# A third buffer for raw expert weights in the dense stage, and seven buffers instead of eight for gathered rows of the second kind

## The chip, the cores and the metric

The kernel runs on one core of one Trainium2 chip. The metric is the device time of one execution in microseconds (us). The engines are named as in the profile: PE is TensorE (PEld its weight loads), DVE is VectorE, ACT is ScalarE, POOL is GpSimd, and SP is SyncE, whose queue issues plain DMAs. POOL issues the gathers.

## The reference, cut to what matters

One layer on 1024 tokens of width 1024: a mixing part (attention and a recurrence) and then the expert part, which this change touches. There are 16384 experts, each with a row `u` and a row `v` of 1024 numbers. Each token takes 8 heads x 16 experts:

```python
q = (xt @ w_query).reshape(TOKEN_BLOCK, PEER_HEADS, 2, PEER_HALF)
s = jnp.einsum('thpd,hpnd->thpn', q, sub_keys)
s_top, i_top = lax.top_k(s, K)
...
idx = jnp.take_along_axis(cand_idx, pos, axis=-1)
g = jax.nn.softmax(best, axis=-1)
u = expert_u[idx]
v = expert_v[idx]
act = jax.nn.gelu(jnp.einsum('td,thkd->thk', xt, u))
return jnp.einsum('thk,thkd->td', g * act, v)
```

## The kernel before, in words

The tokens form eight blocks of 128. Four of them (0, 5, 6, 7) are computed by gathering the chosen rows; the other four, 512 tokens in all, are computed densely, against all 16384 experts with a table of factors G that is zero where an expert was not chosen. The dense stage runs from about 1760 us to the end, and the gathers of token blocks 5, 6 and 7 are woven into it.

The dense stage goes through 128 blocks i of 128 experts. All matmuls use a high and a low part of each operand, three matmuls for one product. For block i the names are:

- `fetch` (line 1358) takes a buffer `raw` of 128x1024 floats (0.5 MB) and issues the DMA that fills it, with u(i) or v(i). `load` also splits it into high and low: a cast on ACT (line 104), a subtraction on DVE (line 105, "sub" below). The raw buffer is free after the subtraction. There are two of them for u and v together.
- `first(i)` is 24 matmuls into `ps_A` with the split `u` (two buffers), and a gelu on ACT into `a` (one buffer, line 1377).
- `weigh(i)` multiplies `a` with the factors on DVE (line 1392) and splits the product into `w` (four buffers): a cast on ACT, a subtraction on DVE.
- `second(g)`, after every fourth block, is 96 matmuls into `ps_y` that use four `w` and four `v`. The split `v` has four buffers, so v(4g+4) can be cast only when second(g) has ended.

PE's order in one group of four blocks is: first(4g+1), first(4g+2), first(4g+3), first(4g+4), second(g). Below, T stands for the end of a second, and the four firsts that follow it are called first 1 to first 4.

The gathers are steps in a list that `pump` works off, some three or four after each first and after each quarter of a second. A step of `gather_u` issues the gather of one row of `u` for 128 tokens (tile `g_u`, four buffers, line 1128) and takes the dot product of an earlier one on DVE (line 1134). A step of `gather_v` issues the gather of one row of `v` (tile `g_v`, GV buffers, line 1174); after every fourth, eight matmuls `g_y` (line 1188) use four gathered rows; the trace shows them as 16 records. Gathers go to POOL in order, and each also waits for the matmul that ended the last point of the pump.

In the first stretch of the dense stage (to about 2190 us) only `u` rows of block 5 are gathered, beside the routing of blocks 6 and 7 on DVE; from 2190 to 3240 us `u` rows and `v` rows by turns; from 3240 us `v` rows of block 7 alone. These are called the u stretch, the mixed stretch and the v stretch below.

On each engine instructions run in the order in which they stand in the program, and a scheduler sets that order when the program is built.

Of the kernel before, what the change touches and what calls it, by code (L numbers as in the profile page):

```python
# [9 lines left out]
F32 = mybir.dt.float32  # L10
# [16 lines left out]
DENSE = tuple(b for b in range(S // 128) if b not in GATHER)  # L27
TD = 128 * len(DENSE)
GC = 16
NGRP = 4  # L30
GU, GV, WB = 4, 8, 4
GUF = 3
BEHIND = 0, 1, 2, 3
FAST = 2
# [19 lines left out]
def b32(ap):  # L54
    return ap.bitcast(F32)
# [29 lines left out]
class Builder:  # L85
# [1013 lines left out]
    def after_part(self, p):  # L1099

        tbs = [tb for tb in range(p * 4, p * 4 + 4) if tb not in LATER]
        tbs = [tb for tb in tbs if tb in GATHER] + [tb for tb in tbs if tb in DENSE]
        rt = {tb: self.soon.pop(tb) if tb in self.soon else self.routed(tb) for tb in tbs}
        dense = sum([rt[tb] + self.table(tb) for tb in tbs if tb in DENSE], [])
        if p == 0:
            self.steps += rt[0] + self.merge(self.gather_u(self.blocks[0]) + self.sooner_v(self.blocks[0]), dense)
        else:
            n = len(rt[4])
            self.steps += dense[:n + 1] + self.merge(dense[n + 1:], rt[BRIDGE])
# [221 lines left out]
    def dense(self, da, db):  # L1331
        nc, I, tc = self.nc, self.I, self.tc
        NB = TD // 128
        groups = [(g, min(g + NGRP, 128)) for g in range(0, 128, NGRP)]
        points = (128 * -(-TD // 512) + len(groups) * NB) * RATE
        rate = (len(self.steps) - self.fast) / (points - self.fast / FAST)
        state = [0.0, self.fast]

        def pump(i, st):
            if state[1] > 0:  # L1340
                self.mark = [st.ins]
                self.pump(FAST)
                state[1] -= FAST
                return
            state[0] += rate
            n = int(state[0])
            state[0] -= n
            self.pump(n)
            self.mark = [st.ins]

        started = set()
        us, acts, Ws, Vs, Gs = {}, {}, {}, {}, {}


        def part(j, dk):
            return h2[j][dk // 4][:, dk % 4, :]

        def fetch(src):
            raw = raws.pop(0) if raws else db.tile([128, 1024], F32, tag="raw", bufs=2, name="raw")
            nc.sync.dma_start(raw, src)  # L1360
            return raw

        def load(src, pool, tag, bufs):
            raw = fetch(src)
            w = pool.tile([128, 2, 1024], F32R, tag=tag, bufs=bufs, name=tag)
            self.split(w[:, 0, :], w[:, 1, :], raw)
            return w

        def first(i):
            u = us.pop(i)  # L1370
            a = acts[i] = a0.pop() if a0 else db.tile([128, TD], F32, tag="a", bufs=1, name="a")
            np_ = -(-TD // 512)
            for c in range(np_):
                cs = slice(c * TD // np_, (c + 1) * TD // np_)
                ps = self.psum([128, TD // np_], "ps_A")
                st = self.lin(ps, u, lambda dk: (part(0, dk)[:, cs], part(1, dk)[:, cs]))
                nc.scalar.activation(a[:, cs], ps, AF.Gelu_apprx_tanh)
                pump(i, st)

        def factors(g):  # L1380
            lo, hi = groups[g]
            Gs[g] = da.tile([128, TD // GC, hi - lo, GC], F32, tag="G", bufs=2, name="Gt")
            nc.sync.dma_start(Gs[g].rearrange("j c i t -> j c (i t)"),
                              self.d_G[:, :, lo:hi, :].rearrange("c j i t -> j c (i t)"))

        def weigh(i):
            g, m = i // NGRP, i % NGRP
            if m == 0 and g + 1 < len(groups):
                factors(g + 1)
            a = acts.pop(i)  # L1390
            a3 = a.rearrange("p (c t) -> p c t", t=GC)
            nc.vector.tensor_tensor(a3, a3, Gs[g][:, :, m, :], op=ALU.mult)
            w = Ws[i] = da.tile([128, 2, TD], F32R, tag="w", bufs=WB, name="w")
            self.split(w[:, 0, :], w[:, 1, :], a)

        def second(g):
            lo, hi = groups[g]
            for tb in range(NB):
                cs = slice(tb * 128, (tb + 1) * 128)
                for hf in range(2):  # L1400
                    ds = slice(hf * 512, (hf + 1) * 512)
                    ps = self.psum([128, 512], "ps_y")
                    st = self.sum3(ps, [(Ws[i][:, 0, cs], Ws[i][:, 1, cs], Vs[i][:, 0, ds], Vs[i][:, 1, ds])
                                        for i in range(lo, hi)])
                    add(tb, hf, ps)
                pump(lo, st)

        def add(tb, hf, ps):
            ds = slice(hf * 512, (hf + 1) * 512)
            if (tb, hf) in started:  # L1410
                nc.vector.tensor_tensor(yac[tb][:, ds], yac[tb][:, ds], ps, op=ALU.add)
            else:
                nc.scalar.copy(yac[tb][:, ds], ps)
            started.add((tb, hf))


        h2 = [[None, None], [None, None]]
        acc = lambda i: db.tile([128, 1024], F32, name=f"yac{i}")

        def half(j, k):  # L1420
            h2[j][k] = db.tile([128, 4, TD], F32R, name=f"dh{j}{k}")

        yac = [acc(i) for i in range(2)]
        raws = [db.tile([128, 1024], F32, tag="raw", bufs=2, name="raw") for _ in range(2)]
        yac.append(acc(2))
        half(0, 0)
        half(1, 0)
        yac.append(acc(3))
        half(1, 1)
        us[0] = load(I["uT"][0], db, "u", 2)  # L1430
        a0 = [db.tile([128, TD], F32, tag="a", bufs=1, name="a")]
        half(0, 1)
        yac += [acc(i) for i in range(4, NB)]

        for j in range(4):
            nc.sync.dma_start(b32(h2[j % 2][j // 2]), self.d_h2T[j % 2][:, (j // 2) * 4:(j // 2) * 4 + 4, :])
        factors(0)
        for i in range(128 + 1):
            if i + 1 < 128:
                us[i + 1] = load(I["uT"][i + 1], db, "u", 2)  # L1440
            if i < 128:
                first(i)
            if i % NGRP == 0 and i or i == 128:
                second((i - 1) // NGRP)
            if i < 128:
                Vs[i] = load(I["expert_v"][i * 128:(i + 1) * 128, :], da, "v", NGRP)
                weigh(i)
        for n in range(NB):
            self.finish(db, DENSE[n], yac[n], "raw", 2)

    def run(self):
        tc = self.tc
# [95 lines left out]
```

## Time and profile before

| what | value |
|---|---|
| time, median of 3 runs | 3584.61 us (3577.67 to 3598.39) |
| the profiled execution's own time | 3616.83 us |
| its span, from the first instruction to the last | 3615.1 us |
| PE busy | 3196.5 us, 88% of the span |
| DVE busy | 2326.8 us, 64% |
| POOL busy | 1375.2 us, 38% |
| ACT busy | 1192.0 us, 33% |
| moved by DMA | 915.68 MB, 253 GB/s over the span |

A busy share is a mean over stages with different limits. Matmuls are pipelined, so each record is longer than the distance from one to the next.

### The profile page before, as it was taken

Reading aid. Unit: us, or ns where it says so; the run is one execution under the profiler, and the core shown is the slowest. Engines: PE = TensorE matmul, PEld = TensorE weight load, DVE = VectorE, ACT = ScalarE, POOL = GpSimd, SP = SyncE. Lnnn points to the kernel's source line nnn. Section 1 sums busy time; section 2 is a strip of 40 time slices with the busy share of each in tenths; the row PEclk is TensorE's granted clock in tenths of the full one; section 3 lists DMA queues with packets and bytes.
Section 4 is the critical chain, followed back from the end, with each engine's and each line's share of the span. In section 5 each row is a group of like instructions: output and inputs, shape, how many; then the busy total and the mean of one; then the engine's idle time right before and its main releaser. Section 6 shows DMA issues by size and latency. Waiting matters only on the chain.

```text
span 3615.1 us, 43218 instructions
## 1 busy us (share of the span) xinstructions
PE 3196.5 (88%) x15408; PEld 2320.3 (64%) x15408; DVE 2326.8 (64%) x5465; ACT 1192.0 (33%) x1860; POOL 1375.2 (38%) x1180
## 2 busy tenths in 40 slices
PE   6899989587878998897697899998989988899997
PEld 4477778465655665565476776665767666666665
DVE  5535557988778644678788776665666565664334
ACT  4437444266425631333332222222222121222121
POOL 0000013134445456431144445555545555554440
PEclk8899999888999999998898999999999999999998
DMA  8422445166776676763788889998999999898995
GB/s 312 161 81 94 135 138 160 58 211 223 265 264 202 230 250 204 242 201 112 247 266 265 288 278 346 340 372 316 351 331 354 344 335 329 312 350 307 346 326 186
DMA packets 392144, 915.68 MB, mean 253 GB/s; under 512 B 162148, under 2 KB 180708, under 8 KB 388088
## 3 DMA queue, kind: packets, MB, share of 16 engines
q0 software_dynamic: 149504, 536.94, 41.9%
q1 hardware_dynamic: 242424, 375.97, 31.9%
q8 instruction: 121, 1.98, 0.2%
q14 instruction: 95, 0.78, 0.1%
HBM read 851.70 MB, written 61.10 MB: 252 GB/s over the span
## 4 chain that ended last, share of the span: by engine, by line
PE 37%; DMA 25%; DVE 19%; issue 11%; ACT 4%; POOL 3%; another core or an unknown queue 0%; SPq 0%; DVEq 0%; POOLq 0%; ACTq 0%
DMA raw<-in_uT 9%; DMA g_u<-in_expert_u,g_ei 5%; DMA raw<-in_expert_v 4%; DVE g_u L1134 3%; PE ps_G L1302 2%; PE ps_y L692 2%; DMA g_u<-in_expert_u,ei 2%; PE ps_y L695 2%; PE g_y L1188 2%; PE ps_y L693 2%; PE h_y L1222 2%; DVE v L105 2%; POOL g_u L1146 2%; PE ps_A L692 1%; PE ps_A L693 1%
## 5 line engine op out<-in xcount | busy, mean ns | idle before, releaser
L1134 DVE CUSTOM_DVE_ANT_0 g_u<-g_u,g_h 128x1024 f32<-128x1024 f32 x384 | 463.9, 1221 | 149.1 <-DMA g_u<-in_expert_u,g_ei 112.2
L692 PE MATMUL ps_A<-dh,u 128*128 128x512 f32 x1024 | 433.3, 423 | 100.6 <-ACT u L104 89.7
L692 PE MATMUL ps_y<-v,w 128*128 128x512 f32 x1024 | 412.9, 403 | 36.2 <-ACT w L104 27.1
L693 PE MATMUL ps_A<-dh,u 128*128 128x512 f32 x1024 | 422.7, 413 | 8.0 <-DMA dh<-d_h2T 8.0
L1128 POOL DMA_INDIRECT g_u<-in_expert_u,g_ei x256 | 298.6, 1167 | 309.3 <-issue 100.8
L693 PE MATMUL ps_y<-v,w 128*128 128x512 f32 x1024 | 404.6, 395 | 0.0
L1174 POOL DMA_INDIRECT g_v<-in_expert_v,g_eT x256 | 284.8, 1112 | 255.0 <-PE g_y L1188 101.4
L1209 POOL DMA_INDIRECT h_v<-in_expert_v,g_eh x256 | 273.6, 1069 | 283.1 <-PE h_y L1222 212.8
L105 DVE TENSOR_TENSOR u<-raw,u 128x1024 fp32r<-128x1024 f32 x128 | 156.7, 1224 | 326.9 <-ACT u L104 308.9
L104 ACT CAST u<-raw 128x1024 fp32r<-128x1024 f32 x128 | 134.0, 1047 | 659.7 <-DMA raw<-in_uT 620.3
L692 PEld LDWEIGHTS ps_A<-dh,u 128*128 128x128 f32 x1024 | 206.9, 202 | 198.0 <-ACT u L104 110.9
L1128 POOL DMA_INDIRECT g_u<-in_expert_u,ei x128 | 163.2, 1275 | 341.9 <-DVE oneA L1295 103.7
L104 ACT CAST v<-raw 128x1024 fp32r<-128x1024 f32 x128 | 134.3, 1049 | 451.7 <-PE ps_y L695 252.4
L695 PE MATMUL ps_y<-v,w 128*128 128x512 f32 x1024 | 279.7, 394 | 0.3 <-DVE w L105 0.3
L692 PEld LDWEIGHTS ps_y<-v,w 128*128 128x128 f32 x1024 | 195.2, 191 | 124.4 <-issue 36.9
L105 POOL TENSOR_TENSOR whl<-wraw,whl 128x1024 fp32r<-128x1024 f32 x16 | 40.6, 2539 | 585.5 <-ACT whl L104 585.4
L1146 POOL DMA_INDIRECT g_u<-in_expert_u,g_ei x128 | 152.6, 1192 | 282.4 <-DVE g_act L1154 116.3
L695 PE MATMUL ps_A<-dh,u 128*128 128x512 f32 x1024 | 253.1, 389 | 0.8 <-DVE u L105 0.8
L104 ACT CAST whl<-wraw 128x1024 fp32r<-128x1024 f32 (+2 forms) x152 | 151.1, 995 | 297.1 <-PE ps_pb L695 55.2
L693 PEld LDWEIGHTS ps_A<-dh,u 128*128 128x128 f32 x1024 | 206.9, 202 | 52.8 <-DMA dh<-d_h2T 9.0
L105 DVE TENSOR_TENSOR whl<-wraw,whl 128x1024 fp32r<-128x1024 f32 (+2 forms) x136 | 155.2, 1142 | 116.1 <-ACT whl L104 112.7
L695 PEld LDWEIGHTS ps_y<-v,w 128*128 128x128 f32 x1024 | 194.6, 190 | 46.3 <-DVE w L105 4.0
(375 smaller groups left out, 6818.7 us busy)
## 6 DMA issues: line engine op xcount, KB each, us to landing
raw<-in_uT SPq DMA_DIRECT2D x128, 512.0 KB
raw<-in_expert_v SPq DMA_DIRECT2D x128, 512.0 KB
wraw<-in_w_in SPq DMA_DIRECT2D x64, 512.0 KB
d_G<-gs SPq DMA_DIRECT2D x64, 512.0 KB
Gt<-d_G SPq DMA_DIRECT2D x32, 1024.0 KB
wada<-in_w_ada SPq DMA_DIRECT2D x32, 512.0 KB
wraw<-in_w_query SPq DMA_DIRECT2D x32, 512.0 KB
x<-in_x SPq DMA_DIRECT2D x16, 512.0 KB
```

The source lines that it names most:

```text
L104: self.nc.scalar.copy(hi, src)
L105: (eng or self.nc.vector).tensor_tensor(lo, src, b32(hi), op=ALU.subtract)
L692: nc.tensor.matmul(ps, lh, rh, start=(n == 0), stop=False)
L693: nc.tensor.matmul(ps, lh, rl, start=False, stop=False)
L695: st = nc.tensor.matmul(ps, ll, rh, start=False, stop=(n == len(terms) - 1))
L1128: st = nc.gpsimd.indirect_dma_start(out=u[:], out_offset=None, in_=I["expert_u"], in_offset=bass.IndirectOffsetOnAxis(ap=g["ei"][:, s:s + ...
L1134: nc.vector.tensor_tensor_reduce(out=u, in0=u, in1=g["h2"], scale=1.0, scalar=0.0, op0=ALU.mult, op1=ALU.add, accum_out=g["act"][:, s:s + 1])
L1146: fetch = lambda s: [nc.gpsimd.indirect_dma_start(out=us.setdefault(k, gp.tile([128, 1024], F32, tag="gu", bufs=GUN, name="g_u"))[:], out_ ...
L1174: st = nc.gpsimd.indirect_dma_start(out=v[:], out_offset=None, in_=I["expert_v"], in_offset=bass.IndirectOffsetOnAxis(ap=g["eT"][:, t:t + ...
L1188: nc.tensor.matmul(g["y"][q * 32:(q + 1) * 32, hf * 512:(hf + 1) * 512], zs[n // 16][:, q, (r % 4) * 32:(r % 4 + 1) * 32], v4[q][:, hf * 5 ...
L1209: nc.gpsimd.indirect_dma_start(out=v[:, m, :], out_offset=None, in_=halves, in_offset=bass.IndirectOffsetOnAxis(ap=g["eh"][hf][:, tok:tok ...
L1222: nc.tensor.matmul(t["y"][q * 32:(q + 1) * 32, :], z[:, q, :], v[q // 2][:, q % 2, :], start=(r == 0), stop=(r == 31), tile_position=(0, q ...
```

## The change

The dense stage gets three raw buffers instead of two. The transfer of u(i+2) is asked for in block i, right behind that of v(i), and not at the head of block i+1; the split of u(i+1) stays where it was. The 4 KB per partition for the third buffer come from the gathered `v` rows: GV is 7 instead of 8, so `g_y` uses rows n-6 to n-3 in the step that issues row n, and not rows n-7 to n-4.

```diff
-GU, GV, WB = 4, 8, 4
+GU, GV, WB = 4, 7, 4
...
-            raw = raws.pop(0) if raws else db.tile([128, 1024], F32, tag="raw", bufs=2, name="raw")
+            raw = raws.pop(0) if raws else db.tile([128, 1024], F32, tag="raw", bufs=3, name="raw")
...
         def load(src, pool, tag, bufs):
-            raw = fetch(src)
+            return halve(fetch(src), pool, tag, bufs)
+
+        def halve(raw, pool, tag, bufs):
             w = pool.tile([128, 2, 1024], F32R, tag=tag, bufs=bufs, name=tag)
             self.split(w[:, 0, :], w[:, 1, :], raw)
             return w
...
+        coming = [fetch(I["uT"][1])]
         for i in range(128 + 1):
             if i + 1 < 128:
-                us[i + 1] = load(I["uT"][i + 1], db, "u", 2)
+                us[i + 1] = halve(coming.pop(), db, "u", 2)
             if i < 128:
                 first(i)
             if i % NGRP == 0 and i or i == 128:
                 second((i - 1) // NGRP)
             if i < 128:
-                Vs[i] = load(I["expert_v"][i * 128:(i + 1) * 128, :], da, "v", NGRP)
+                raw = fetch(I["expert_v"][i * 128:(i + 1) * 128, :])
+                if i + 2 < 128:
+                    coming.append(fetch(I["uT"][i + 2]))
+                Vs[i] = halve(raw, da, "v", NGRP)
                 weigh(i)
...
-            self.finish(db, DENSE[n], yac[n], "raw", 2)
+            self.finish(db, DENSE[n], yac[n], "raw", 3)
```

The change also moves instructions, since the scheduler places them anew. The first place is ACT in the u stretch, from the cast of u(22) on; the rows are v(20), w(20), v(21), a(21), u(23), and so on. Before:

```order
L104 CAST u<-raw 128x1024
L104 CAST v<-raw 128x1024
L104 CAST w<-a 128x512
L104 CAST v<-raw 128x1024
L1377 ACTIVATE a<-ps_A 128x512
L104 CAST u<-raw 128x1024
L104 CAST w<-a 128x512
L104 CAST v<-raw 128x1024
L1377 ACTIVATE a<-ps_A 128x512
L104 CAST u<-raw 128x1024
```

and of the changed kernel, at the same place:

```order
L104 CAST u<-raw 128x1024
L104 CAST v<-raw 128x1024
L104 CAST w<-a 128x512
L104 CAST v<-raw 128x1024
L1379 ACTIVATE a<-ps_A 128x512
L104 CAST u<-raw 128x1024
L104 CAST v<-raw 128x1024
L104 CAST w<-a 128x512
L1379 ACTIVATE a<-ps_A 128x512
L104 CAST u<-raw 128x1024
```

Here v(22) has moved ahead of w(21), and u(23) still stands ahead of v(22).

The second place is ACT in the mixed stretch, from the cast of u(66) on; the rows are u(66), v(64), w(64), v(65) and v(66), a(65), u(67), and so on. Before:

```order
L104 CAST u<-raw 128x1024
L104 CAST v<-raw 128x1024
L104 CAST w<-a 128x512
L104 CAST v<-raw 128x1024 x2
L1377 ACTIVATE a<-ps_A 128x512
L104 CAST u<-raw 128x1024
L104 CAST w<-a 128x512
L1377 ACTIVATE a<-ps_A 128x512
L104 CAST u<-raw 128x1024
```

and of the changed kernel:

```order
L104 CAST u<-raw 128x1024
L104 CAST v<-raw 128x1024
L104 CAST w<-a 128x512
L104 CAST v<-raw 128x1024 x2
L1379 ACTIVATE a<-ps_A 128x512
L104 CAST u<-raw 128x1024
L104 CAST w<-a 128x512
L104 CAST v<-raw 128x1024
L1379 ACTIVATE a<-ps_A 128x512
L104 CAST u<-raw 128x1024
```

Here the cast of v(67) has come between w(65) and a(66), and so ahead of the cast of u(68), which stood ahead of it before.

## Rows read from the trace of the kernel before

**Rows 1.** Windows: busy us (records) by engine, granted clock, DMA share, GB/s.
```profile
1760.00:2190.00 430.00, 361.25 (x1473) 289.18 (x1473) 339.71 (x634) 114.47 (x146) 174.88 (x140) 0.92 0.87 284
2190.00:3240.00 1050.00, 960.97 (x4443) 690.73 (x4444) 648.20 (x965) 228.17 (x292) 581.38 (x493) 0.96 0.95 339
3240.00:3540.00 300.00, 299.12 (x1519) 198.18 (x1518) 116.92 (x159) 64.21 (x82) 139.65 (x135) 1.00 0.93 330
2340.00:2460.00 120.00, 112.34 (x540) 79.93 (x539) 78.39 (x117) 28.46 (x37) 73.08 (x63) 0.99 1.02 371
```

**Rows 2.** Waits of PE, 1760 to 2190 us: total, times, longest.
```profile
PE ps_A L692 <- ACT u L104: 47.1, 16, 7.6
```

**Rows 3.** Waits of PE, 1760 to 1815 us, a part of that stretch.
```profile
PE ps_A L692 <- ACT u L104: 13.8, 5, 4.6
```

**Rows 4.** Waits of PE, 2190 to 3240 us.
```profile
PE ps_A L692 <- ACT u L104: 42.2, 18, 5.9
...
PE g_y L1188 <- DMA g_v<-in_expert_v,eT: 3.3, 2, 1.9
```

**Rows 5.** Waits of PE, 3240 to 3600 us.
```profile
PE g_y L1188 <- DMA g_v<-in_expert_v,g_eT: 0.4, 2, 0.2
```

**Rows 6.** Timeline of DVE in the mixed stretch: start, duration; sub of v(64).
```profile
2677.51 1.22 DVE L105 TENSOR_TENSOR v<-raw,v 128x1024 fp32r<-128x1024 f32 x1
```

**Rows 7.** Timeline of SP's queue, the same group: transfers of u(67) and u(68).
```profile
2678.75 0.33 SPq L1360 DMA_DIRECT2D raw<-in_uT  x1
...
2691.04 0.33 SPq L1360 DMA_DIRECT2D raw<-in_uT  x1
```

**Rows 8.** Timeline of ACT, the same group: casts of v(66), u(67), u(68).
```profile
2688.70 1.05 ACT L104 CAST v<-raw 128x1024 fp32r<-128x1024 f32 x1 [9.97 <-issue]
...
2690.14 1.03 ACT L104 CAST u<-raw 128x1024 fp32r<-128x1024 f32 x1
...
2698.90 1.04 ACT L104 CAST u<-raw 128x1024 fp32r<-128x1024 f32 x1 [4.86 <-DMA raw<-in_uT]
```

**Rows 9.** Timeline of PE, the same group: the start of first(68).
```profile
2699.99 0.50 PE L692 MATMUL ps_A<-dh,u 128*128 128x512 f32 x1 [1.17 <-ACT u L104]
```

**Rows 10.** Timeline of DVE in the u stretch: subs of v(20) and v(21).
```profile
2063.80 1.21 DVE L105 TENSOR_TENSOR v<-raw,v 128x1024 fp32r<-128x1024 f32 x1
...
2065.53 1.21 DVE L105 TENSOR_TENSOR v<-raw,v 128x1024 fp32r<-128x1024 f32 x1
```

**Rows 11.** Timeline of SP's queue, the same group: transfer of u(23).
```profile
2065.03 0.33 SPq L1360 DMA_DIRECT2D raw<-in_uT  x1
```

**Rows 12.** Timeline of ACT, the same group: gelu of block 21, cast of u(23).
```profile
2065.70 0.60 ACT L1377 ACTIVATE a<-ps_A 128x512 f32<-128x512 f32 x1 [7.49 <-DVE w L105]
2072.03 1.04 ACT L104 CAST u<-raw 128x1024 fp32r<-128x1024 f32 x1 [5.73 <-DMA raw<-in_uT]
```

**Rows 13.** Timeline of PE, the same group: the starts of first(23) and first(24).
```profile
2073.12 0.79 PE L692 MATMUL ps_A<-dh,u 128*128 128x512 f32 x1 [7.63 <-ACT u L104]
...
2080.90 0.39 PE L692 MATMUL ps_A<-dh,u 128*128 128x512 f32 x1
```

**Rows 14.** Timeline of PE in the v stretch: the matmuls on gathered rows.
```profile
3347.24 2.47 PE L1188 MATMUL g_y<-g_v,g_z 128*32 128x512 f32 x16
...
3355.32 1.92 PE L1188 MATMUL g_y<-g_v,g_z 128*32 128x512 f32 x16
...
3362.88 1.92 PE L1188 MATMUL g_y<-g_v,g_z 128*32 128x512 f32 x16
```

**Rows 15.** Timeline of POOL, the same place: two of the gathers.
```profile
3339.40 0.93 POOL L1174 DMA_INDIRECT g_v<-in_expert_v,g_eT  x1 [0.30 <-issue]
...
3357.50 0.94 POOL L1174 DMA_INDIRECT g_v<-in_expert_v,g_eT  x1 [3.42 <-PE g_y L1188]
```

**Rows 16.** Timeline of PE in the mixed stretch: a late gathered row.
```profile
2330.21 2.63 PE L1188 MATMUL g_y<-g_v,g_z 128*32 128x512 f32 x9 [1.91 <-DMA g_v<-in_expert_v,eT]
```

**Rows 17.** Timeline of POOL, the same place: the gather of that row.
```profile
2324.51 1.04 POOL L1174 DMA_INDIRECT g_v<-in_expert_v,eT  x1 [0.30 <-issue]
```

More of the change, by code (lines that the diff above doesn't have):

```diff
@@ L1423, in dense @@
         yac = [acc(i) for i in range(2)]
-        raws = [db.tile([128, 1024], F32, tag="raw", bufs=2, name="raw") for _ in range(2)]
+        raws = [db.tile([128, 1024], F32, tag="raw", bufs=3, name="raw") for _ in range(3)]
         yac.append(acc(2))
```

## The prediction

> **What bounds the kernel now.** I read the windows by stage first, because the change touches only what lies behind 1760 us. PE is the engine that sets the end there: 360 of 430 us busy in the u stretch, 961 of 1050 in the mixed stretch, 299 of 300 in the v stretch [rows 1]. The reader is to see that in the v stretch nothing can be won on PE, and that what is missing before it is some 70 and 90 us, beside a granted clock of 0.92 and 0.96. The DMA share is 0.87 and 0.95, so transfers are near their rate, but not at it: one stretch of 120 us ran at 371 GB/s against 339 as the mean [rows 1].
>
> Then the waits of PE in the same stretches. Nearly all of the waiting for something that the change touches is one line, a first that waits for the ACT cast of its `u`: 47.1 us in the u stretch [rows 2], of which 13.8 lie at its very start [rows 3], 42.2 in the mixed stretch, beside 3.3 for gathered rows [rows 4]. In the v stretch there is next to none, and 0.4 us of waiting for gathered rows [rows 5]. Together some 90 us can be won from `u` at the outside, and the gathered rows, which get a buffer less, cost nearly nothing today.
>
> Last the timeline, for what a late `u` waits for. In the mixed stretch the second ends, v(64) is at last cast, its subtraction ends at 2677.51 + 1.22 = 2678.73 [rows 6], and in that moment the transfer of u(67) starts [rows 7]. The cast of v(66) comes at 2688.70, 1.05 long, and when its subtraction has ended the transfer of u(68) starts at 2691.04; it lands 7.86 us later, at the cast at 2698.90 [rows 7, 8], and first(68) starts at 2699.99 [rows 9]. So after each second two transfers run one after the other through one raw buffer, because v(4g) and its follower hold both buffers while the second runs. In the u stretch it is the same with u(23): v(20)'s subtraction ends at 2065.01 [rows 10], the transfer starts at 2065.03 [rows 11], the cast comes at 2072.03, 7.0 us later [rows 12], and first(23) has waited 7.63 us [rows 13].
>
> **The change, part by part.** No bytes are added or removed. In each block two lines on SP's queue change their places, and the cast on ACT is put in a new order. No instruction gets longer, so what the edit costs or gives is waits alone.
>
> The u stretch. With three buffers u(4g+3) takes the buffer of u(4g+2) and is fetched while the second runs. Where its cast stands ahead of that of v(4g+2), as in the first piece of order shown, it waits only for the gelu of block 21, which ends at 2065.70 + 0.60 = 2066.30 [rows 12]. Cast by 2067.3, first(23) starts at about 2067.4 and not at 2073.12 [rows 13]. Now v(22) is what is late: it follows v(20) in its buffer, so it starts at 2065.0, lands at 2072.0 (7.0 us, as u(23) took), is cast by 2073.05 and subtracted by 2074.3. The subtraction of w(21) stands behind it (estimated at 0.7, somewhat over half of a 128x1024 one [rows 10]), 2075.0; gelu of block 22 until 2075.6; cast of u(24) until 2076.65; first(24) at 2076.8, where it was 2080.90 [rows 13]. That is 4.1 us won. In the new order three of the seven groups of this stretch have `u` ahead in this way: 3 x 4.1, **-12**. In the other four the cast of v stands ahead, and I put them at nothing, by the next paragraph. Bounds: 0, and the 47.1 - 13.8 = 33.3 us of waiting in this stretch behind its start [rows 2, 3].
>
> The start of the stretch. u(2) is asked for a block earlier, when nothing gathers yet. I take one of the five waits as gone, the longest at 4.6 [rows 3]: **-5**, between 0 and -13.8.
>
> The mixed stretch. In the second piece of order the cast of v(67) stands ahead of the gelu of block 66 and of u(68). In the new plan of buffers v(4g+2) follows v(4g), and v(4g+3) follows v(4g+2): again two transfers one after the other, but now of `v`, and u(68), though it landed long before, stands behind them on ACT. Worked for this group: 2678.75 + 7.0 = 2685.75 for v(66) to land; cast 1.05 and subtraction 1.22 [rows 6, 8], 2688.0; v(67) 7.9 us later, 2695.9; its cast 1.05, a gelu 0.60, the cast of u(68) 1.04, and first(68) at about 2698.7 against 2699.99 [rows 9]. That is 1.3 us won where 1.17 was the wait in the trace, with 7.0 us for a transfer in a stretch whose own u(67) and u(68) needed more. Two of the 18 groups have `u` ahead, as in the u stretch: 2 x 4.1. For the rest I take a loss of 0.2 each, since a cast of v and a gelu (1.65 us) are in the chain that were not, and they use up what the earlier start gives. Sum **-5**. Bounds: -42.2 [rows 4] if `u` really is no longer waited for, and +26 (16 x 1.65) if each group loses the cast and the gelu.
>
> Seven buffers for gathered rows. The matmuls `g_y` of a step use four rows, and seven buffers hold three further ones: the last row of the next four can be gathered only when the previous `g_y` has ended. In the v stretch a `g_y` started at 3355.32, the gather behind it went out at 3357.50 [rows 14, 15], 2.2 us later, and the next `g_y` started at 3362.88 [rows 14]: 5.4 us for the row to arrive, and some 0.7 more until the fourth row is used (estimate, a third of the 1.92 us that one `g_y` takes). So 6.1 us. How long a gather takes, the trace shows from both sides: 5.7 us in the mixed stretch, from 2324.51 to the matmul that waited for it at 2330.21 [rows 16, 17]; and in the v stretch about 9.1, from 3339.40 [rows 15] to the later part of a `g_y` that started at 3347.24 and ran 2.47 instead of 1.92 [rows 14]. That one was the last of its burst; the row in question would be the first of one, ahead of three gathers of 0.93 + 0.30 each [rows 15], 3.7 us less: 5.4. So between -0.7 (nothing) and 3.0 per `g_y`. I take 0.5, nearer to the lower end because of its place in the burst. Of the 32 `g_y` of this stretch I count 23 that follow the one before as closely as this: 23 x 0.5, **+11** (0 to +69). Here PE has no other gaps that could swallow it: 299 of 300 us are busy [rows 1]. The cover that is gone is one gathered row.
>
> In the mixed stretch `g_y` stands further apart. PE waited 3.3 us in two places [rows 4], with 1.9 the longest [rows 16]. The change takes a row of reserve from all of them; I take **+4**, between 0 and +12 (about six further waits of 1.9).
>
> Sum: -12 - 5 - 5 + 11 + 4 = -7 us. Against the profiled execution's 3616.8 us (1.7 us over its span) that is 3610. The median of the runs is 3584.6, 0.9% below the profiled one, and the same 7 us from it give **3578 us**.
>
> **The rivals.**
>
> *The wait for `u` really goes in the mixed stretch* (B). For it: the third buffer allows three transfers at once, and transfers did run at 371 GB/s for 120 us; the transfers then overlap and none needs 7.9 us alone. With it the clock comes back, 0.96 against 0.99 in that faster window [rows 1]: 3% of 1050 us is 31 us at most. Against it: the order on ACT shown above. What transfers allow: 1050 x 339 / 371 = 959 us, so 91 us are to be had, more than the 42 + 31. Taking 42 and half of the 31, with the 17 of the u stretch and its start, and +15 for the gathered rows: -60, 3525 us (3500 to 3545).
>
> The Trainium skill speaks against this rival: "DMA: Bandwidth & Descriptors", Specifications, has a limit of about 358 GB/s from HBM for a core, and says of transfers from HBM that this side binds. By it the mixed stretch could shrink to 994 us, an estimate from the page's figure, so by 56 us and not by 91. The 371 GB/s of the window above, over 120 us [rows 1], disagree, and the measurement decides.
>
> *The wait only changes its name* (C). The buffer is one more, but ACT works in program order, and v(4g+2) takes the place of u(4g+3) in all groups, those of the u stretch too, because the transfer is longer with three in flight. Then the 17 us are not won and the mixed stretch gives nothing: +15, 3600 us. For it speaks a DMA share of 0.95 [rows 1], against it the 7.63 us ahead of first(23) [rows 13], which a transfer during the second simply takes away.
>
> *Slower, by the seventh buffer* (D). If a gathered row of the v stretch takes 9.1 us even as the first of its burst, each of the 23 `g_y` loses 3.0, +69; with +12 in the mixed stretch, and -22 from the three terms of `u`, +59: 3644 us. It decides from a latency of 6.1 + 22/23, about 7.1 us, on, where the loss eats the gain. For it: the DMA share of 0.93 in that stretch [rows 1]. Against it: the first gather of a burst has no others ahead of it on POOL.
>
> **How the numbers follow.** Chances: as worked 0.50 (own range 3560 to 3597), B 0.20, C 0.12, D 0.18. A change of 0.5%, 18 us, is about what a measurement of this kernel can tell from none. As worked, some 0.12 lies below 3567, 0.34 within, 0.04 above 3602; B is faster; C lies 0.08 within and 0.04 above; D 0.16 above and 0.02 within. So faster 0.32, same 0.44, slower 0.24. The range 3520 to 3640 leaves out the better half of B and the worse half of D, about 0.2 together.
>
> **What the changed profile would show.** In the u stretch PE's wait for the cast of `u` falls from 47.1 to about 30 us. In the mixed stretch it stays at 35 to 45 us, but on ACT the wait ahead of it is no longer for the raw of `u` but for that of `v`; if it falls below 20 us, B is right. In the v stretch PE waits for `g_v` 5 to 20 us; 50 or more is D. What makes me wrong most easily is how long transfers take when three of them and a gather share the queues: at 6 us instead of 7.0 and 7.9 every chain above is 2 to 3 us shorter and B comes near; at 9 us C.

## The result, and the profile after

The changed kernel took 3532.61 us (median of 3 runs, 3528.13 to 3542.11) against 3584.61: a ratio of 0.9858, 95% interval 0.9823 to 0.9893, 52 us less. The profiled execution has a span of 3526.3 us and a time of its own of 3528.13 us. The profile before was 88.8 us longer, and not all of that is the change: its dense stage began at 1760.2 us, that of the changed kernel at 1735.4, and in the eight further profiles of this study, of kernels whose edits all lie behind that point, at 1737.9 to 1758.0. So 24.8 us are left out of the comparison. What lies behind compares by stage, from the timeline (first matmul of `first(0)`; start of the second in which the mixed stretch begins, and of the one in which it ends; last matmul of `ps_y`):

| us | u stretch | mixed stretch | v stretch | rest to the end |
|---|---|---|---|---|
| before | 426.4 | 1048.5 | 359.5 | 20.5 |
| after | 418.4 | 983.3 | 374.7 | 14.5 |
| difference | -8.0 | **-65.2** | +15.2 | -6.0 |

The four differences add up to 64 us, for one profile of each kernel; the medians are 52 us apart. The same mixed stretch took 980.9 and 996.0 us in two kernels with three raw buffers that are shown below, so a single profile leaves some 15 us open there.

Windows of the changed kernel, cut at these places; the columns are those of [rows 1]:

```profile
1735.00:2154.00 419.00, 356.39 (x1468) 286.34 (x1469) 339.27 (x636) 114.77 (x146) 174.51 (x136) 0.92 0.87 288
2154.00:3137.00 983.00, 935.97 (x4449) 680.22 (x4448) 645.47 (x960) 225.26 (x290) 594.08 (x493) 0.98 1.00 362
3137.00:3437.00 300.00, 290.47 (x1424) 189.47 (x1421) 115.39 (x156) 61.52 (x80) 128.72 (x126) 0.99 0.91 314
```

The mixed stretch does the same work in 65 us less, PE's clock there is 0.98 instead of 0.96, and the transfers run at 362 GB/s over the whole of it. In the v stretch PE is no longer busy throughout. The waits of PE in the three stretches of the changed kernel, which answer to [rows 2], [rows 4] and [rows 5]:

```profile
PE ps_A L692 <- ACT u L104: 39.7, 11, 9.4
...
PE ps_A L692 <- ACT u L104: 46.1, 23, 4.2
PE ps_y L692 <- ACT w L104: 0.9, 1, 0.9
...
PE g_y L1188 <- DMA g_v<-in_expert_v,g_eT: 9.8, 11, 3.0
```

The wait for `u` is no smaller in the mixed stretch than it was: 46.1 us against 42.2. The 65 us are not from there. Two rows that stood in the same view of before, 2190 to 3240 us, and on which the prediction built nothing, say where half of them are from:

```profile
PE ps_y L692 <- ACT w L104: 25.4, 13, 4.3
PE ps_y L692 <- DVE yac L1411: 9.1, 4, 4.0
```

Second waited for `w`, the last factor that it uses, and for `ps_y` to be added up. One wait of 1.0 us lies behind the end of the stretch; of the other 33.5 us, 0.9 is left. The timeline of ACT before, at the second that starts at 2930.9 us, shows why `w` was late:

```profile
2928.16 0.59 ACT L1377 ACTIVATE a<-ps_A 128x512 f32<-128x512 f32 x1
2934.12 1.04 ACT L104 CAST u<-raw 128x1024 fp32r<-128x1024 f32 x1 [5.38 <-DMA raw<-in_uT]
2935.07 0.61 ACT L104 CAST w<-a 128x512 fp32r<-128x512 f32 x1
```

The gelu of block 83 is done at 2928.75. The next instruction on ACT is the cast of u(85), which nobody needs before the second has ended, some 30 us later. Its transfer has not landed, so ACT stands for 5.38 us, and the cast of w(83) behind it comes at 2935.07, though the product that it reads was there at 2931.3. PE waits, and works more slowly behind the wait (the last line is a window, with the columns of [rows 1]):

```profile
2935.74 0.79 PE L692 MATMUL ps_y<-v,w 128*128 128x512 f32 x1 [3.36 <-ACT w L104]
2936.34 0.63 PE L693 MATMUL ps_y<-v,w 128*128 128x512 f32 x1
2935.00:2941.00 6.00, 5.26 (x12) 4.13 (x13) 5.46 (x9) 1.29 (x3) 0.00 (x0) 0.50 1.04 384
```

The granted clock of these 6 us is 0.50, the lower of its two levels, and a matmul that took 0.39 us ahead of the wait takes 0.63.

The sums of `ps_y` were late by the next transfer, that of u(4g+6). DVE and PE before, in the second that starts at 3113.7 us:

```profile
3137.30 1.22 DVE L105 TENSOR_TENSOR u<-raw,u 128x1024 fp32r<-128x1024 f32 x1 [13.23 <-ACT u L104]
3138.44 0.68 DVE L1411 TENSOR_TENSOR yac<-yac,ps_y 128x512 f32<-128x512 f32 x1
3139.17 0.66 PE L692 MATMUL ps_y<-v,w 128*128 128x512 f32 x1 [4.01 <-DVE yac L1411]
```

The subtraction is that of u(98). It waits for its cast, the cast waits for its transfer, and a sum of `ps_y` that PE needs stands behind it on DVE. In all four waits of that row it is the subtraction of u(4g+6) that stands there.

In the changed kernel, in the group of u(85) again, ACT has the same order, and the cast of u(85) takes no wait, because its transfer went out at 2851.67 and had landed:

```profile
2860.53 0.60 ACT L1379 ACTIVATE a<-ps_A 128x512 f32<-128x512 f32 x1 [1.18 <-DVE w L105]
2861.02 1.04 ACT L104 CAST u<-raw 128x1024 fp32r<-128x1024 f32 x1
2862.22 0.62 ACT L104 CAST w<-a 128x512 fp32r<-128x512 f32 x1 [0.15 <-DVE a L1394]
```

In the summary of ACT's waits in the mixed stretch it is one row, first before (2187 to 3235 us), then after (2154 to 3137 us):

```profile
ACT u L104 <- DMA raw<-in_uT: 398.1, 60, 22.0
```

```profile
ACT u L104 <- DMA raw<-in_uT: 26.6, 13, 3.6
```

Only a part of the first row harms `w`: before, the cast of u(4g+5) stood ahead of that of w(4g+3) in 17 of the 18 groups and waited 76.6 us there in all. In the changed kernel it stands ahead in all 18, and 0.9 us is left.

ACT is busy for a fifth of that stretch and looks as if it had time to wait. It has not: what stands behind the waiting cast is on PE's path.

This is how the 65 us add up. PE's idle time in the mixed stretch fell from 89.9 to 47.0 us, by 43: 32.6 are the two waits of second, some 14 are four smaller rows that are gone, and 4 went to a longer wait for `u`. Its busy time fell from 958.1 to 936.0 us for the same matmuls, by 22: the granted clock stood at its lower level for 82 us of the stretch before, and for 31 us after.

### The profile page after: what moved, and what is told of

The parts are those of the page before. It is cut to its first block, busy times and chain, and to the rows that moved or that the text cites. A ratio compares the mean times of both kernels' runs of the same rounds, so it can differ in the third digit from the quotient of the medians.

```text
span 3526.3 us, 43247 instructions
## 1 busy us (share of the span) xinstructions
PE 3172.5 (90%) x15408; PEld 2310.4 (66%) x15408; DVE 2322.1 (66%) x5465; ACT 1187.7 (34%) x1860; POOL 1384.7 (39%) x1180
## 5 line engine op out<-in xcount | busy, mean ns | idle before, releaser
L692 PE MATMUL ps_A<-dh,u 128*128 128x512 f32 x1024 | 425.6, 416 | 85.7 <-ACT u L104 85.7
L693 PE MATMUL ps_A<-dh,u 128*128 128x512 f32 x1024 | 416.4, 407 | 7.9 <-DMA dh<-d_h2T 7.9
L692 PE MATMUL ps_y<-v,w 128*128 128x512 f32 x1024 | 406.3, 397 | 4.4 <-ACT w L104 4.4
L693 PE MATMUL ps_y<-v,w 128*128 128x512 f32 x1024 | 400.5, 391 | 0.0
L692 PEld LDWEIGHTS ps_A<-dh,u 128*128 128x128 f32 x1024 | 202.8, 198 | 178.5 <-ACT u L104 110.5
L695 PE MATMUL ps_y<-v,w 128*128 128x512 f32 x1024 | 275.5, 391 | 0.0
L1413 DVE TENSOR_TENSOR yac<-yac,ps_y 128x512 f32<-128x512 f32 x248 | 165.6, 682 | 135.2 <-PE ps_y L695 135.2
L695 PE MATMUL ps_A<-dh,u 128*128 128x512 f32 x1024 | 253.5, 390 | 0.2 <-DVE u L105 0.2
L105 DVE TENSOR_TENSOR v<-raw,v 128x1024 fp32r<-128x1024 f32 x128 | 156.3, 1221 | 143.8 <-ACT v L104 143.7
L693 PEld LDWEIGHTS ps_A<-dh,u 128*128 128x128 f32 x1024 | 202.7, 198 | 51.4 <-DMA dh<-d_h2T 8.9
```

The source lines that it names most:

```text
L105: (eng or self.nc.vector).tensor_tensor(lo, src, b32(hi), op=ALU.subtract)
L692: nc.tensor.matmul(ps, lh, rh, start=(n == 0), stop=False)
L693: nc.tensor.matmul(ps, lh, rl, start=False, stop=False)
L695: st = nc.tensor.matmul(ps, ll, rh, start=False, stop=(n == len(terms) - 1))
```

## The experiments

The theory after the result: **the third buffer brings u(4g+5) early, which frees the queue of ACT ahead of w(4g+3)**, and the wait for `u` that is left comes from the order of casts on ACT. That u(4g+6) does the same on DVE for the sums of `ps_y` is read from the traces; no run changes that transfer alone. Rivals: the earlier request did it, the new places of the gathers did it, or more transfers in flight did it as such. Times of different chips stand by their ratio to before on the same chip (before: 3592.17 us for the first four, 3607.50 us for the last four).

**Seven gathered rows alone.** Before, with `GV = 7`.

```diff
-GU, GV, WB = 4, 8, 4
+GU, GV, WB = 4, 7, 4
```

> The kernel before with seven buffers for gathered second rows and nothing else. If the seventh buffer only costs, as in the v stretch of the changed kernel, where the matmuls on gathered rows took some 17 us longer in all, it is 10 to 25 us slower than before, about 3600 us, and second still waits about 24 us for w in the mixed stretch. If the new places of the gathers are what made the mixed stretch shorter, it is 20 us or more faster than before.

Measured: 3623.84 us, ratio 1.0078 (1.0052 to 1.0105). By stage, the v stretch took 382.5 us instead of 359.5, the mixed one 1056.2 instead of 1048.5. It is some 28 us slower by the ratio, a little more than expected. The seventh buffer only costs, and the places of the gathers give nothing: PE's wait of the second for `w` is still there (21.6 us from 2190 to 3240).

**The third buffer without the earlier request.** The loop of before, with three raw buffers and `GV = 7`.

```diff
-tag="raw", bufs=2, name="raw")
+tag="raw", bufs=3, name="raw")
```

> Third raw buffer and seven gathered rows, but u(i+1) is asked for where the kernel before asks for it. The order of the built program is nearly that of the changed kernel. If the third buffer alone makes the transfers early, the time is that of the changed kernel within 0.5%, 3515 to 3550 us. If the request two blocks ahead matters, it is 3565 to 3600 us.

Measured: 3538.86 us, ratio 0.9848 (0.9801 to 0.9894), that of the changed kernel. The u stretch took 413.1, the mixed stretch 980.9, the v stretch 375.1 us. On SP the 256 transfers of u and v stand in the same sequence in the kernel before, the changed one and this one, v(i) and then u(i+2): the scheduler had u(i+2) there already, and what kept it back was the buffer. The earlier request in the code does next to nothing.

**The cast of w ahead of that of u(4g+5).** Before, with that order forced.

```diff
                 us[i + 1] = load(I["uT"][i + 1], db, "u", 2)
+                if i % NGRP == 0 and i:
+                    self.after(self.cast, [wcast[0].ins])
```

> The kernel before, two raw buffers and eight gathered rows, with one order forced on ACT: the cast of u(4g+5) comes behind the cast of w(4g+3). If second was late because w(4g+3) stood behind a cast that waited for its transfer, the wait of second for w in the mixed stretch falls from 24 us to under 5, and the time by 20 to 45 us, to 3540 to 3565 us, with transfers as late as before. If the gain came from more transfers in flight, the time stays within 10 us of before.

Measured: 3612.47 us, ratio 1.0051 (1.0018 to 1.0085), a miss: neither outcome came. The wait for `w` did go, but another grew in its place. Waits of PE in this kernel, 2190 to 3240 us:

```profile
PE ps_y L692 <- DVE yac L1413: 29.3, 5, 6.8
...
PE ps_y L692 <- ACT w L104: 0.9, 3, 0.4
```

The cast of u(85) comes behind `w` now and waits 1.7 us. What holds PE up is u(86), that is u(4g+6): its transfer goes out at 2913.48, when u(85) has been subtracted, its cast waits for it until 2933.25, its subtraction on DVE waits for the cast, and the sums of `ps_y` stand behind that. ACT, DVE and PE of this kernel at that place:

```profile
2933.25 1.04 ACT L104 CAST u<-raw 128x1024 fp32r<-128x1024 f32 x1 [20.56 <-DMA raw<-in_uT]
```

```profile
2934.33 1.23 DVE L105 TENSOR_TENSOR u<-raw,u 128x1024 fp32r<-128x1024 f32 x1 [15.46 <-ACT u L104]
2935.47 0.68 DVE L1413 TENSOR_TENSOR yac<-yac,ps_y 128x512 f32<-128x512 f32 x1
```

```profile
2936.20 0.80 PE L692 MATMUL ps_y<-v,w 128*128 128x512 f32 x1 [6.03 <-DVE yac L1413]
```

So the expectation was too narrow: two late transfers hold up two queues, that of u(4g+5) the one of ACT and that of u(4g+6) the one of DVE. In all five waits for `yac` of this row it is the subtraction of u(4g+6) that stands ahead; there were four such waits, of 9.1 us, before. To free the one queue by force left the other stalled, and longer. With the third buffer both transfers are early, and both waits go. By itself the run does not speak against more transfers in flight as the cause; the next one does, in part.

**u(4g+5) late again.** The changed kernel, in which that transfer alone waits for the subtraction of u(4g+4).

```diff
                     coming.append(fetch(I["uT"][i + 2]))
+                    if i % NGRP == NGRP - 1:
+                        self.after(self.asked, [usub.ins])
```

> The changed kernel, but the transfer of u(4g+5) alone may start only when u(4g+4) has been subtracted, as it did before. In 14 of 18 groups of the mixed stretch its cast still stands ahead of that of w(4g+3). If that wait was the cost, second waits 15 us or more for w again in the mixed stretch and the time is 20 to 45 us above the changed kernel, 3555 to 3575 us. If it is the other transfers that gained, it is within 10 us of the changed kernel.

Measured: 3579.56 us, ratio 0.9963 (0.9942 to 0.9985), against 0.9858 for the changed kernel: 1.05% or 38 us of the 52 are gone, give or take 15. The run without the earlier request, on the same chip, was 41 us faster than this one. The wait of second for `w` is back, from 0.9 us (2190 to 3240 us):

```profile
PE ps_A L692 <- ACT u L104: 47.1, 24, 5.3
PE ps_y L692 <- ACT w L104: 18.5, 7, 3.9
```

The wait for `u` is that of the changed kernel, 46.1. So one of the four transfers of `u` in a group carries most of the gain in time. By stage it is less clear: against the profile of the changed kernel the mixed stretch is 23.4 us longer (1006.7), the u stretch 5.1 and the v stretch 7.4. Only 23 of the 65 us of the mixed stretch are back. In 5 of its 18 groups the scheduler has put the cast of u(4g+5) behind that of w(4g+3), and u(4g+6) is still early: PE does not wait for `yac` here. For the rest of the 65 us no run separates u(4g+6) from more transfers in flight as such.

**An eighth row for the last token block.** The changed kernel; every eighth gathered v row of token block 7 uses a `g_u` buffer, which are idle in the v stretch.

```diff
+                if g["tb"] == GATHER[-1] and n % 8 == 7:
+                    v = vs[n] = gp.tile([128, 1024], F32, tag="gu", bufs=GU, name="g_v")
```

> The changed kernel, in which every eighth gathered v row of the last token block takes a g_u buffer, idle by then; so eight rows fit again in the v stretch and seven elsewhere. If the seventh buffer is what made that stretch longer (matmuls on gathered rows 61 + 14 us before, 75 + 16 after), it is 12 to 20 us faster than the changed kernel, 3512 to 3521 us. If the transfers through three raw buffers did it, it stays within 5 us of the changed kernel's 3533 us.

Measured: 3552.28 us, ratio 0.9841 (0.9795 to 0.9887). That can't be told from the changed kernel's 0.9858; in its profile the v stretch took 362.6 us instead of 374.7, 12 us less, and the mixed stretch, whose code is the same, 996.0 instead of 983.3, for which the runs give no reason. The 12 to 20 us that were expected do not show in its time. Two kernels of one chip make the comparison clearer (below).

**Casts of u ahead of those of v.** The changed kernel, with the casts of v(4g+2) and v(4g+3) behind those of u(4g+3) and u(4g+4).

```diff
                 Vs[i] = halve(raw, da, "v", NGRP)
+                if i % NGRP > 1 and i + 1 < 128:
+                    self.after(self.cast, [ucast.ins])
```

> The changed kernel with the casts of v(4g+2) and v(4g+3) forced behind those of u(4g+3) and u(4g+4) on ACT. If the wait for u that is left in the mixed stretch (46 us) is that of the u cast behind a cast of v whose transfer is late, it falls below 25 us and the time by 20 to 45 us from the changed kernel's 3533, to 3488 to 3513 us. If the late v then holds up the second instead, the wait of second for w grows by as much and the time stays within 10 us.

Measured: 3496.34 us, ratio 0.9704 (0.9654 to 0.9754), 1.5% below that of the changed kernel, some 55 us, more than expected. In the mixed stretch, which took 931.2 us, the row of PE's wait for `u` is gone, and the window is full:

```profile
2175.00:3103.00 928.00, 925.00 (x4428) 671.27 (x4428) 642.95 (x958) 229.91 (x290) 609.20 (x491) 1.00 1.04 381
```

`v` is not late for the second: the wait for `w` is 0.8 us. So the 46 us that the change left are those of a u that lies in its buffer behind a v that doesn't. Against the changed kernel the mixed stretch is 52 us shorter: 44 us of PE's idle time, and 8 us of its busy time, at a granted clock of 1.00 throughout.

**Both.** The two edits above together.

> Both of the two edits, u ahead of v on ACT and the eighth row of the last token block in a g_u buffer. If both theories hold, their gains add up: 3475 to 3500 us. If the first doesn't, 3510 to 3525 us.

Measured: 3480.23 us, ratio 0.9646 (0.9603 to 0.9690). Beside the kernel without the eighth row, on the same chip, that is 16 us less, and the v stretch took 358.9 us instead of 373.3. This kernel beats both that the study began with.

**Four raw buffers**, three for gathered u rows, and the eighth row.

```diff
-GU, GV, WB = 4, 7, 4
+GU, GV, WB = 3, 7, 4
...
-tag="raw", bufs=3, name="raw")
+tag="raw", bufs=4, name="raw")
```

> Four raw buffers, with three instead of four for gathered u rows, and the eighth v row of the last token block in a g_u buffer. v(4g+2) then follows u(4g+2) in its buffer and is fetched during the second, so no two transfers run one after the other behind it. If that chain is the wait for u that is left, it falls below 20 us in the mixed stretch and the time to 3470 to 3500 us. If the transfers have no rate left or three buffers for u rows hold DVE up, it is 3510 us or more.

Measured: 3576.22 us, ratio 0.9924 (0.9892 to 0.9955). In the mixed stretch the wait for the cast of `u` is as good as gone (0.3 us), as the chain said. But the time is that of the second outcome, 24 us more than the kernel with three raw buffers and the eighth row on the same chip. PE waits for gathered rows, 35 us where the changed kernel has none and [rows 4] has 3.3, and DVE's wait for `g_u` in the mixed stretch went from 211.4 us in the changed kernel to 312.4:

```profile
PE g_y L1192 <- DMA g_v<-in_expert_v,eT: 22.8, 20, 3.2
PE g_y L1192 <- DMA g_v<-in_expert_v,g_eT: 12.5, 10, 2.9
```

Whether the fourth buffer for gathered u rows is missed, with a late u gather on POOL that holds up the v gather behind it, or the rate of the transfers is used up, these runs don't separate.

## Why the prediction was right or wrong

The time, 3532.6 us, lies in the range of 3520 to 3640 us and near the 3525 of rival B, but well below the forecast of 3578 and outside its own range of 3560 to 3597. Neither reason was the one: B expected the wait for `u` to fall below 20 us, and it is 46.1. That the time lies in the range is luck. The sum had -5 us for the mixed stretch, and the range reached low enough only for the sake of B, whose mechanism did not come.

**The step that failed** is the second paragraph of the prediction, "nearly all of the waiting for something that the change touches is one line", and with it the bound of -42.2 us for the mixed stretch. Measured -65.2, outside the bounds. By the view of [rows 4] 34.5 us of waiting of the second stood beside the 42.2, under `w` and `yac`, names that the diff doesn't touch. They hang on the change by the order on ACT and DVE, where the cast of u(4g+5) stands ahead of that of w(4g+3), and the subtraction of u(4g+6) ahead of a sum of `ps_y`. The prediction followed u(4g+3) and u(4g+4), which first needs soon, and left out u(4g+5) and u(4g+6), which nobody needs soon. In the 18 groups of the stretch the time from the end of a second to the start of the next went from 556.4 to 541.7 us, and the seconds themselves from 492.0 to 441.6. Of these 50 us 32.6 are waits of PE. The rest is matmuls that take less time each, at a clock that rose from 0.96 to 0.98. So "what the edit costs or gives is waits alone" failed too: over the whole stretch the same matmuls kept PE busy for 22 us less. The prediction had put the clock under B alone, as what comes back with the wait for `u`; here it rose though that wait stayed.

**The order of casts** was right. The prediction said that in the mixed stretch the wait for `u` stays at 35 to 45 us and is then one for the raw of `v`. It is 46.1, a little above, and putting u ahead of v removed it.

**"In each block two lines on SP's queue change their places"** was wrong: the code changes, the built sequence of transfers does not, and the run without the earlier request has the same time.

**The u stretch and its start** were to give 12 and 5 us; they gave 8.0 in all, 5.2 of them up to the start of the first second (55.3 us before, 50.1 after), and so 2.8 behind it. In the run without the earlier request the stretch was 13.3 us shorter than before, so single profiles leave some 5 us open. The term of 12 was mis-sized, and not by the count of groups: in the order that ran, `u` is ahead of v(4g+2) in five of the seven, not in three. first(23) does start without a wait, as worked, but first(19) waits 9.4 us for a cast of `u`, where the longest was 7.6 [rows 2].

**The seventh buffer** was forecast at +11 in the v stretch and measured +15.2 there, and 14.4 us came back with the eighth row. The place in the burst does not save the row. Matmuls on gathered rows in the changed kernel, to set beside [rows 14], and POOL at the same place:

```profile
3297.96 1.93 PE L1188 MATMUL g_y<-g_v,g_z 128*32 128x512 f32 x16
3305.48 1.38 PE L1188 MATMUL g_y<-g_v,g_z 128*32 128x512 f32 x4
3307.07 1.04 PE L1188 MATMUL g_y<-g_v,g_z 128*32 128x512 f32 x2 [0.21 <-DMA g_v<-in_expert_v,g_eT]
3308.66 1.90 PE L1188 MATMUL g_y<-g_v,g_z 128*32 128x512 f32 x10 [0.54 <-DMA g_v<-in_expert_v,g_eT]
```

```profile
3297.02 0.94 POOL L1174 DMA_INDIRECT g_v<-in_expert_v,g_eT  x1 [0.30 <-issue]
3300.14 0.94 POOL L1174 DMA_INDIRECT g_v<-in_expert_v,g_eT  x1 [2.18 <-PE g_y L1188]
```

The second of these steps is torn in three, from 3305.48 to 3310.56, 5.1 us instead of 1.9. Its fourth row is the one of 3300.14, the first of its burst, and by the order of the rows it is what the matmuls of 3308.66 waited for: 8.5 us, where I had taken 5.4 as the lower end and 6.1 as what there was. The third row, of 3297.02, took 10.05. But a few pay, up to 5.5 us each, and not all a little: of the 25 steps of token block 7 that start within 11 us of the one before, 14 took less than 0.2 us more. For the mixed stretch +4 was taken; there the wait for gathered rows, 3.3 us in [rows 4], has no row in the changed kernel. With two raw buffers and seven gathered rows it was 8.1 us from 2190 to 3240.

**The end** was left out of the sum. The last lines of the kernel use the raw buffers too; with three of them the time from the last matmul to the end is 14.5 us and not 20.5. It was 13.9 to 14.5 us in the six kernels with three, 18.6 to 20.5 in the three with two, and 7.0 with four.

**The rate of transfers.** The prediction took 371 GB/s as what is to be had, 959 us for the mixed stretch. It took 983 at 362 GB/s, and 931 in the run with u ahead, at 381 GB/s. The Trainium skill's limit of about 358 GB/s for a core ("DMA: Bandwidth & Descriptors", Specifications) does not agree with these two stretches, and the measurement decides. By the same page, under Bandwidth, that figure is a core's share when both cores of the pair stream, and this kernel runs on one; read whole, the page speaks less against rival B than the prediction had it. No run here found where the rate ends.

## What to carry to other kernels

Where a change makes a transfer early or late, list what stands behind its first reader on that engine, and behind the second reader on the next, before asking who needs the data: here a cast that nobody waited for stalled PE through the cast queued behind it on ACT, and a subtraction that nobody waited for through the sum queued behind it on DVE. Read every row of the waits of the engine that sets the end, those under names that the diff doesn't touch too, and follow each back to the queue. Count what the waits do to the clock as well: of the 65 us a third was PE's busy time. And look at the built order, not at the code, for what a request in another place moves: here the buffer did it all, and a constraint on the order of two casts gave as much again.

## What the runs showed of the hardware

The work ahead of the dense stage ended anywhere between 1735 and 1760 us in ten profiles; a difference of 25 us between two single profiles says nothing there. Transfers of 0.5 MB together with gathers of 4 KB rows ran at 381 GB/s for 928 us, with a DMA share of 1.04. Behind a wait of PE of 3.4 us the granted clock stood at 0.50 for some 6 us, and matmuls took 0.63 us and not 0.39: that wait cost more than its length. And a row gathered as the first of its burst took 8.5 us, not much less than the 9.1 that I had read for a last one.
